# A two-layer hybrid decoder step: queries and keys stored by heads in DRAM, and the mixer's norm, bonus and gate made a stream of their own

## The chip, the core and the metric

The kernel runs as one program on one core of a Trainium2 chip. Five engines work beside each other and are tied by semaphores: TensorE (PE, with its weight loads as PEld), VectorE (DVE), ScalarE (ACT), GpSimd (POOL) and SyncE (SP), which here only issues DMAs. The metric is the device time of one execution in microseconds, lower is better. The granted clock is the share of TensorE's full clock that the chip gave (1.0 is 2.4 GHz, 0.5 is 1.2 GHz).

## The reference, cut to what matters

A prompt of 1024 positions and eight decode rows pass through two layers. In each layer one projection gives eight attention heads and eight RWKV-7 heads, whose outputs are joined, projected, normed and sent through a feed-forward block.

```python
def hybrid_layer(x, pos, x_prev, wkv0, kv_buf, v_first, lp):
    p = x @ lp['w_in']                       # q|k|v of 8 heads x 64, then r|k|v and LoRA columns
    q, k, v = ...                            # (B, T, 8, 64) each
    q, k = rope(q, pos), rope(k, pos)        # rotates the two 32-halves of each head
    att = dilated_attention_prompt(q, k, v)  # windows/dilations (128,1),(512,4),(2048,16), merged
    att = att * rsqrt(mean(att**2, -1) + RMS_EPS) * lp['att_gain']
    z = token_shift(p[..., ATT_COLS:], ...)
    rw, v_first, S_T = rwkv7_time_mix(z, v_first, wkv0, lp)
    mix = concatenate([att, rw], -1) @ lp['w_out']
    x1 = layer_norm(ALPHA * x + mix, ...)
    h = square(relu(x1 @ lp['w_ff_up'])) @ lp['w_ff_down']
    return layer_norm(ALPHA * x1 + h, ...), ...

def rwkv7_time_mix(z, v_first, wkv0, lp):
    ...
    g = sigmoid(g_lo) @ lp['gate_up']                       # gate
    def step(S, inp):                                       # per position, state S 64 x 64 per head
        sa = einsum('bhvk,bhk->bhv', S, a_t)
        S = S * w_t + sa * b_t + v_t * k_t                  # outer products
        return S, einsum('bhvk,bhk->bhv', S, r_t)
    S_T, y = lax.scan(step, wkv0, xs)
    y = (y - mean(y)) * rsqrt(var(y) + GN_EPS) * gn_g + gn_b   # per head: the norm
    y = (y + sum(r * k * bonus_rk, -1) * v) * g                # bonus, gate
    return y, v_first, S_T
```

## The kernel before, in words

**Halves and pairs.** Positions are cut into two halves of 512 (h = 0, 1; the decode rows ride with h = 1), and heads into four pairs p of 128 partitions (two heads of 64). The work of a layer l and half h is: the projection (`in_proj`), attention for four pairs, the RWKV mixer for four pairs in units of 256 positions (two units u per pair, 32 units in all, numbered s), then `half`: output projection, layer norm, feed-forward, layer norm.

**Dense work.** Every dense product is done in three passes (tiles xh/xl or hh/hl times wh/wl, lines 370 to 372, PSUM tile `dps`), in three PSUM banks tagged "d". ACT makes wh from each raw weight tile (line 343) and DVE makes wl (line 344); ACT also issues the weight loads.

**The order of PE's work** is written out when the program is built. Streams (Python generators) hand in pieces with a planned cost, a planned hold on a PSUM bank and a planned latency. `Streams.step` multiplies holds and latencies by a stream's slack: 1.2 in its first half-layer, 2.2 later (`SLK`, read through `R.phase`, which a stream sets by `R.enter`; a stream that never does so keeps 1.2). `Streams.run` always takes the first stream in the list that is ready at the planned time; dense work stands last and fills the rest. PE executes this list in order. The other engines' orders are chosen by the tile scheduler, and they too run in order: an instruction that waits holds up all behind it on its engine, and on SP a DMA that waits holds up all DMAs behind it.

**PSUM banks.** "r": one bank, for the mixer's second stage; "o": two, for that stage's outputs; "d": three, dense; "a": two, attention, the mixer's first stage and the rest.

**The mixer.** `stage1` makes a unit's operands: gates, norms, the decay products (AR, Wd), the triangular matrices (LB), and their inverse, for which POOL solves 16 x 16 blocks (lines 1209, 1211) between two trips through DRAM (`d_el`). It also makes the bonus term bv. `stage2` finishes the inverse (T1, pX: bank r), forms the products pO in the two o banks, and runs the chain over four blocks of 64 positions (St, pz, Z: bank r). Its last part is the norm, bonus and gate of y: `pgm` (the mean over each head, and the gate's product from `gs` and `gup`), `pgv` (the variance), three DVE operations and the store to `d_rw`, with both PE pieces in bank r. `stage1` of unit s starts after that last part of unit s-2 (note "u2").

**Attention's operands.** `in_proj` brings queries and keys (tile `qe`) out of PSUM in an order of partitions that suits the rotation: first halves of both heads, then second halves. It stores them as they are in `d_qkv` (line 638, one DMA of 128 x 512). `att_load` fetches them for the next pair, 64 partitions at a time, and puts a head's two halves together through the access pattern of the load:

```python
def heads(src):
    return src.rearrange("(f d r) t -> d f r t", f=2, d=2)
def stage(src, hd, n):
    t = ap_.tile([128, HB], F32, tag="stg", bufs=2, name="stg")[:, :n]
    for x in range(2):
        S.dma_start(t[64 * x:64 * x + 64], heads(src)[hd])
    return t
```

Here d is the head, f the half of the head, r the row in it; `stg` has two buffers. Each `stg` is then copied by ACT (qS line 1522, kS line 1526) and subtracted from by POOL (qL line 1523, kS line 1527). In the second half `qf` and `kf` (lines 1514, 1515) are loaded in the same way.

Of the kernel before, what the change touches and what calls it, by code (L numbers as in the profile page):

```python
# [10 lines left out]
F32 = mybir.dt.float32  # L11
# [10 lines left out]
NB = 8  # L22
DEPTH = 2
# [224 lines left out]
def body(ctx, tc, I, O):  # L248
# [303 lines left out]
    def in_proj(l, h, hook=None, tail=None, then=None):  # L552
# [61 lines left out]
        for kind, p in proj_order()[1:]:  # L614
            if kind == "a" and p == 3 and then is not None:
                yield from then()
            for j in range(3):
                w = W.take()
                if kind == "z":
                    ev = z_ev(p, j)  # L620
                    for c0, n in ck:
                        yield from dense([(w, 128, c0, n)], K8, xhc, xlc, ev)
                    continue
                seq = (2 * l + h) * 4 + p
                if j == 1 and seq > 0:
                    yield after("post", seq - 1)
                t = ap_.tile([128, HN[1]], F32, tag="qe", bufs=2, name="qe")

                def eva(it, pt):
                    _, _, c0, n = it  # L630
                    (V.tensor_copy if c0 else A.copy)(t[:, c0:c0 + n], pt[:, :n])
                for c0, n in CK[h]:
                    yield from dense([(w, 128, c0, n)], K8, xhc, xlc, eva)
                if j == 0 and h == 1:
                    t8 = ap_.tile([128, 5, 8], F32, tag="t8", name="t8")
                if j < 2:
                    rope(t, HN[h], tabs)
                    S.dma_start(d_qkv[l][h][p, j], t[:, 0:HB])
                    if j == 1:
                        S.dma_start(O["k_p"][l, p, :, h * HB:h * HB + HB], t[:, 0:HB])  # L640
                if h == 1 and j == 0:
                    if p == 0:
                        sq[l] = (rq.tile([128, 4, 32], F32, tag="q2", name="q2"), rq.tile([128, 4, 8], F32, tag="kn", name="kn"))
                        G.memset(sq[l][0], 0.0)
                    G.memset(t8[:, 1:4, :], 0.0)
                    for hd in range(2):
                        G.tensor_scalar(sq[l][0][:, p, hd:16:2], t[:, HB:HN[1]], C("hm")[:, hd:hd + 1], None, op0=ALU.mult)
                elif h == 1:
                    G.tensor_scalar(t8[:, (0, 4)[j - 1], :], t[:, HB:HN[1]], 1.0, None, op0=ALU.mult)
                    if j == 1:  # L650
                        G.tensor_scalar(sq[l][1][:, p, :], t[:, HB:HN[1]], 1.0, None, op0=ALU.mult)
            if kind == "a":
                qe[seq] = (l, h, p, t, t8 if h == 1 else None)
                note("qe", seq)
            note(kind, l, h, p)
# [427 lines left out]
    def stage1(l, h, p, u, s, lw, out):  # L1083
# [46 lines left out]
        if last:  # L1130
            yield (430, ("a", 1100), 0, "a")
            decode_terms(l, p, th, dup)
            yield (400, ("a", 700), 2000, "a")
        else:
            yield (860, ("a", 1100), 2000, "a")
        pb = bank("a", "pn")
        PE.matmul(pb[:, :n], C("blk"), sq, start=True, stop=True)
        if last:
# [102 lines left out]
            PE.transpose(pb[:, cc * 128:cc * 128 + 128], AR[:, tb, o:o + 128], ident)  # L1241
        A.copy(TV[:, :, :, 0, :], pb.rearrange("p (c h x) -> p c h x", c=4, h=2))
        yield (440, ("a", 900), 0, "a")
        pb = bank("a", "pbn")
        PE.matmul(pb[:, :n], C("blk"), bp, start=True, stop=True)
        bv = tmp("bv", bufs=2)
# [33 lines left out]
                    PE.matmul(pb[r, o + i * 64:o + i * 64 + 64], lt, rh, start=True, stop=True)  # L1280
        return pb[:, o:o + 256].rearrange("p (i t) -> p i t", t=64)

    def stage2(l, h, p, u, s, st, Z, Zp, gup, gs):

        AR, Wd, LB, TV, X, XT, bv, _ = st

# [84 lines left out]
        if h == 1 and u == NU - 1:  # L1371
            yield (200, ("r", 650), 900, "r")
            pz = bank("r", "pzf")
            for hd in range(2):
                hs = slice(64 * hd, 64 * hd + 64)
                PE.matmul(pz[hs, 0:64], Z[hs, :], istk[hs, :], start=True, stop=True)
            PE.matmul(pz[:, 64:72], gup, gs[:, UN:UN + NB], start=True, stop=True)
            Zo = rp.tile([128, 64], F32, tag="Zo", name="Zo")
            V.tensor_copy(Zo, pz[:, 0:64])
            S.dma_start(O["wkv_p"][l, 0, 2 * p:2 * p + 2].rearrange("h v k -> (h v) k"), Zo)  # L1380
            V.tensor_copy(dd["gsd"][:, p, :], pz[:, 64:72])
        yield (300, ("r", 700), 1500, "r")
        pb = bank("r", "pgm")
        PE.matmul(pb[:, 0:256], C("blk"), y, start=True, stop=True)
        PE.matmul(pb[:, 256:512], gup, gs[:, 0:256], start=True, stop=True)
        V.scalar_tensor_tensor(y, pb[:, 0:256], -1.0 / 64, y, op0=ALU.mult, op1=ALU.add)
        gg = rq.tile([128, 4, 64], F32, tag="T1", name="gg").rearrange("p a b -> p (a b)")
        A.copy(gg, pb[:, 256:512])
        sq = rq.tile([128, 4, 128], F32, tag="FG", name="gq").rearrange("p a b -> p (a b)")[:, 0:256]
        A.activation(sq, y, AF.Square)  # L1390
        yield (860, ("r", 1000), 1800, "r")
        pb = bank("r", "pgv")
        PE.matmul(pb[:, 0:256], C("blk"), sq, start=True, stop=True)
        A.activation(sq, pb[:, 0:256], AF.Ln, bias=epsc[:, 1:2], scale=1.0 / 64)
        A.activation(sq, sq, AF.Exp, scale=-0.5)
# [1 line left out]
        V.scalar_tensor_tensor(y, y, pv(l, "gnb", p), bv[:, 0:256], op0=ALU.add, op1=ALU.add)  # L1397
        V.tensor_tensor(y, y, gg, op=ALU.mult)
        S.dma_start(d_rw[l][h][p, :, u * UN:u * UN + UN], y)
        yield (430, ("r", 2000), 0, None)  # L1400

    def unit(l, h, p, u):
        return ((l * 2 + h) * 4 + p) * NU + u

    units = {}

    def stage1_stream():
        for l in range(DEPTH):
            for h in range(2):
                R.enter("s1", 2 * l + h)  # L1410
                yield after("lo", l, h, lat=3500)
                yield after("init")
                if h == 1:
                    for nm, k in (("dvt", 5), ("bvd", 4)):
                        dd[nm] = rq.tile([128, k, 8], F32, tag=nm, name=nm)
                for p in range(4):
                    yield after("z", l, h, p, lat=3500)
                    pc = slice(128 * p, 128 * p + 128)
                    dup = rp.tile([65, 128], F32, tag="dup", name="dup")
                    S.dma_start(dup[0:64, :], I["decay_up"][l, :, pc])  # L1420
                    S.dma_start(dup[64:65, :], I["decay_base"][l:l + 1, pc])
                    iup = rp.tile([128, 128], F32, tag="iup", name="iup")
                    S.dma_start(iup[64:128, :], I["iclr_up"][l, :, pc])
                    if l > 0:
                        S.dma_start(iup[0:32, :], I["vres_up"][l - 1, :, pc])
                    for u in range(NU):
                        s = unit(l, h, p, u)
                        if s >= 2:
                            yield after("u2", s - 2)
                        out = []  # L1430
                        yield from stage1(l, h, p, u, s, (dup, iup), out)
                        units[s] = out[0]
                        R.times["s1", s] = max(out[0][-1], R.now + 2000)
                if h == 1:
                    yield from decode(l)
                    note("dec", l)

    def stage2_stream():
        Zp = rp.tile([128, 4, 64], F32, tag="Zp", name="Zp")
        for l in range(DEPTH):  # L1440
            for h in range(2):
# [1 line left out]
                if h == 1:  # L1443
                    dd["gsd"] = rq.tile([128, 4, 8], F32, tag="gsd", name="gsd")
                for p in range(4):
                    gup = rp.tile([128, 128], F32, tag="gup", name="gup")
                    for u in range(NU):
                        s = unit(l, h, p, u)
                        yield after("s1", s)
                        if u == 0:  # L1450
                            S.dma_start(gup, I["gate_up"][l, :, 128 * p:128 * p + 128])
                        n = HN[h] - u * UN if u == NU - 1 else UN
                        gs = rp.tile([128, 264], F32, tag="gs", name="gs")
                        S.dma_start(gs[:, :n], d_lo[l][h][2, :, u * UN:u * UN + n])
                        yield (0, None, 0, "r")
                        yield from stage2(l, h, p, u, s, units.pop(s), None if h == 0 and u == 0 else Zp[:, p, :], Zp, gup, gs)
                        note("u2", s)
                    note("s2", l, h, p)

    def att_stream():  # L1460
# [27 lines left out]
    def att_load(l, h, p):  # L1488
# [2 lines left out]

        qS, qL, kS = [], [], []

        def heads(src):
            return src.rearrange("(f d r) t -> d f r t", f=2, d=2)

        def stage(src, hd, n):
            t = ap_.tile([128, HB], F32, tag="stg", bufs=2, name="stg")[:, :n]
            for x in range(2):
                S.dma_start(t[64 * x:64 * x + 64], heads(src)[hd])  # L1500
            return t

        def byres(t):
# [5 lines left out]
        qf = kf = None  # L1509
        if h == 1:  # L1510
            qf, kf = (ap_.tile([128, HB], F32, tag=x, name=x) for x in ("qf", "kf"))
            for hd in range(2):
                hs = slice(64 * hd, 64 * hd + 64)
                S.dma_start(qf[hs], heads(d_qkv[l][1][p, 0])[hd])
                S.dma_start(kf[hs], heads(d_qkv[l][0][p, 1])[hd])
        for hd in range(2):
            hs, ls = slice(64 * hd, 64 * hd + 64), slice(64 - 64 * hd, 128 - 64 * hd)
            q = ap_.tile([128, HB], F32R, tag=f"q{hd}", name="qS")
# [271 lines left out]

    R.work = WORK
    R.add("s2", stage2_stream(), SLK)
    R.add("s1", stage1_stream(), SLK)
    R.add("att", att_stream(), SLK)
    R.add("post", post_stream(), SLK)
# [64 lines left out]
```

## Time and profile before

| | |
|---|---|
| median of 3 runs | 3555.35 us (3549.26 to 3558.99) |
| profiled execution | 3560.94 us, its span 3559.1 us |
| mean granted TensorE clock | 0.949 |
| PE busy | 3202.7 us (90%) |
| DVE, ACT, POOL busy | 2055.5 us (58%), 1448.3 us (41%), 979.3 us (28%) |
| DMA queue q1 (SP's) | 245064 packets, 175.92 MB |

A row of a view of groups has the line of the kernel, engine, operation, tiles written and read, shapes, count, and times; a bracket at the end of a row of the timeline is the idle time of that engine just before the instruction and what ended it. "SPq" and "ACTq" are the engines' queues that issue DMAs.

### The profile page before, as it was taken

To read this page: it belongs to the slowest core of one execution; us is meant where nothing else is said; L and a number is where in the kernel's file an instruction comes from. 1 tells how busy PE (TensorE), PEld (TensorE's weight loads), DVE (VectorE), ACT (ScalarE), POOL (GpSimd) and SP (SyncE) were. 2 spreads that over 40 slices of the span, in tenths; PEclk is the share of its full clock that TensorE was granted. 3 is DMA by queue.
4 is the path that set the end of the run, shared out by engine and by line. 5 is a ranking of instruction groups with operands and counts; after the bars stand their busy time and mean duration, and the time that the engine had idled before them with its cause. 6 is when DMAs were issued, how large, how long until landed. Compare 5 with 4: busy or idle time off the path is not lost. (4 is left out here: it accounts for less than half of the span.)

```text
span 3559.1 us, 65853 instructions
## 1 busy us (share of the span) xinstructions
PE 3202.7 (90%) x24732; PEld 2697.6 (76%) x24732; DVE 2055.5 (58%) x4703; ACT 1448.3 (41%) x3266; POOL 979.3 (28%) x1841
## 2 busy tenths in 40 slices
PE   8788897977999998888999999797797999889998
PEld 6567776765777687677899998685675677789998
DVE  4455554764554664567565457465764564685556
ACT  4345333443343344344443336343443333453334
POOL 2324233531111421435211113334412121340012
PEclk9899998988999999998999999898898999999999
DMA  7334343433443335442333235344243343333332
GB/s 219 107 113 124 115 115 103 129 95 99 117 112 85 106 97 163 139 150 68 86 98 92 80 98 154 117 126 133 71 118 100 111 113 91 117 101 91 94 90 84
DMA packets 366533, 393.55 MB, mean 111 GB/s; under 512 B 141848, under 2 KB 219112, under 8 KB 366216
## 3 DMA queue, kind: packets, MB, share of 16 engines
q10 hardware_dynamic: 121152, 213.44, 20.9%
q1 hardware_dynamic: 245064, 175.92, 16.9%
q8 instruction: 195, 3.19, 0.4%
q14 instruction: 122, 1.00, 0.1%
HBM read 325.30 MB, written 63.97 MB: 109 GB/s over the span
## 5 line engine op out<-in xcount | busy, mean ns | idle before, releaser
L370 PE MATMUL dps<-xh,wh 128*128 128x256 f32 (+3 forms) x2984 | 1006.9, 337 | 31.0 <-ACT xh L758 15.0
L371 PE MATMUL dps<-xl,wh 128*128 128x256 f32 (+3 forms) x2984 | 956.8, 321 | 10.4 <-DVE xl L759 8.6
L372 PE MATMUL dps<-xh,wl 128*128 128x256 f32 (+3 forms) x2984 | 953.3, 319 | 1.2 <-DVE wl L344 1.0
L344 DVE TENSOR_TENSOR wl<-wr,wh 128x512 fp32r<-128x512 f32 (+1 forms) x772 | 581.8, 755 | 501.3 <-ACT wh L343 485.6
L343 ACT CAST wh<-wr 128x512 fp32r<-128x512 f32 (+1 forms) x772 | 475.1, 616 | 844.4 <-PE dps L371 777.8
L370 PEld LDWEIGHTS dps<-xh,wh 128*128 128x128 f32 x2984 | 576.6, 193 | 106.4 <-issue 31.0
L371 PEld LDWEIGHTS dps<-xl,wh 128*128 128x128 f32 x2984 | 576.8, 193 | 46.3 <-DVE xl L759 12.5
L372 PEld LDWEIGHTS dps<-xh,wl 128*128 128x128 f32 x2984 | 575.6, 193 | 41.0 <-DVE wl L344 2.6
L370 PE MATMUL dps<-hh,wh 128*128 128x512 f32 (+2 forms) x1600 | 536.1, 335 | 5.4 <-DVE hh L941 3.6
L371 PE MATMUL dps<-hl,wh 128*128 128x512 f32 (+2 forms) x1600 | 513.1, 321 | 4.5 <-DVE hl L830 3.3
L372 PE MATMUL dps<-hh,wl 128*128 128x512 f32 (+2 forms) x1600 | 512.0, 320 | 0.0
L370 PEld LDWEIGHTS dps<-hh,wh 128*128 128x128 f32 x1600 | 303.5, 190 | 45.2 <-issue 17.7
L371 PEld LDWEIGHTS dps<-hl,wh 128*128 128x128 f32 x1600 | 304.1, 190 | 22.6 <-DVE hl L830 4.1
L372 PEld LDWEIGHTS dps<-hh,wl 128*128 128x128 f32 x1600 | 303.9, 190 | 22.6
L1209 POOL TENSOR_TENSOR tm<-BL,XB 32x15 f32<-32x15 f32 (+7 forms) x480 | 153.0, 319 | 496.5 <-DMA BL<-d_el 375.9
L973 DVE TENSOR_TENSOR t<-dps,t 128x256 f32<-128x256 f32 (+1 forms) x240 | 123.6, 515 | 161.1 <-PE dps L372 160.7
L1211 POOL TENSOR_TENSOR XB<-XB,tm 32x15 f32<-32x15 f32 (+7 forms) x480 | 154.6, 322 | 34.4
L726 POOL TENSOR_TENSOR ln<-ln,lsq 128x256 f32<-128x256 f32 (+1 forms) x112 | 91.2, 814 | 232.5 <-ACT lsq L724 229.9
L941 DVE CAST hh<-rl 128x256 fp32r<-128x256 f32 (+2 forms) x200 | 74.4, 372 | 108.6 <-ACT rl L940 105.4
L939 ACT ACTIVATE rl<-dps 128x256 f32<-128x256 f32 (+2 forms) x200 | 88.4, 442 | 102.2 <-PE dps L372 89.9
L715 POOL TENSOR_TENSOR t<-t,ln 128x256 f32<-128x256 f32 (+1 forms) x32 | 28.1, 913 | 352.1 <-ACT ln L709 352.1
L370 PE MATMUL dps<-hh,xh 128*128 128x256 f32 (+1 forms) x368 | 112.6, 306 | 13.3 <-DVE t L1006 7.2
(345 smaller groups left out, 5098.0 us busy)
## 6 DMA issues: line engine op xcount, KB each, us to landing
wr<-in_w_ff_up ACTq DMA_DIRECT2D x272, 256.0 KB
wr<-in_w_ff_down ACTq DMA_DIRECT2D x256, 256.0 KB
wr<-in_w_in ACTq DMA_DIRECT2D x220, 256.0 KB
stg<-d_qkv SPq DMA_DIRECT2D x128, 128.0 KB
wr<-in_w_out ACTq DMA_DIRECT2D x64, 256.0 KB
z<-d_z SPq DMA_DIRECT2D x24, 384.0 KB
d_qkv<-qe SPq DMA_DIRECT2D x32, 256.0 KB
kvc<-in_cache_k SPq DMA_DIRECT2D x32, 256.0 KB
```

The lines of the kernel that those rows point to most:

```text
L343: self.copies.append(A.copy(h[:, :, :m], w[:, :, :m]))
L344: V.tensor_tensor(lo[:, :, :m], w[:, :, :m], h.bitcast(F32)[:, :, :m], op=ALU.subtract)
L370: PE.matmul(p[:m, :n], wh[:, wk % 4, :m], hi, start=(i == 0), stop=False)
L371: PE.matmul(p[:m, :n], wh[:, wk % 4, :m], lo, start=False, stop=False)
L372: PE.matmul(p[:m, :n], wl[:, wk % 4, :m], hi, start=False, stop=(i == last))
L715: G.tensor_tensor(t, t, self.cm[:, c0:c0 + n], op=ALU.subtract)
L726: G.tensor_tensor(s2, s2, sq, op=ALU.add)
L939: A.activation(r, p[:, :n], AF.Relu)
L941: V.tensor_copy(hh[:, c0:c0 + n], r)
L973: V.tensor_tensor(to, p[:, :n], to, op=ALU.add)
L1209: G.tensor_tensor(tv, bc(BL[:, 17 * j + 1:17 * j + 2], [(1, m), (0, j + 1)]), bc(XB[:, 16 * j:16 * j + 1], [(0, m), (1, j + 1)]), op=ALU.mult)
L1211: G.tensor_tensor(xv, xv, tv, op=ALU.add)
```

## The change

Two things are changed. First, the store of rotated queries and keys is cut into four DMAs of 32 partitions each, which put the two halves of a head beside each other in DRAM; the loads of `stg` then read 64 rows that lie together, and `qf` and `kf` are one load of 128 rows each. Second, the norm, bonus and gate leave `stage2` and become a generator `normed`, driven by a new stream "norm" that stands behind "s2" in the list and takes banks tagged "o" instead of "r". The end of the chain of unit s is noted as "ch". `stage1` no longer waits for "u2" of unit s-2 at its start; it waits for "ch" of s-2 before it writes AR and Wd and for "u2" of s-2 before it writes bv. The gate is copied into `gs` in place of a buffer of its own. The norm stream never calls `R.enter`.

```diff
                 if j < 2:
                     rope(t, HN[h], tabs)
-                    S.dma_start(d_qkv[l][h][p, j], t[:, 0:HB])
+                    for f in range(2):
+                        for d in range(2):
+                            a, b = 64 * f + 32 * d, 64 * d + 32 * f
+                            S.dma_start(d_qkv[l][h][p, j, b:b + 32], t[a:a + 32, 0:HB])
@@ stage1
+        if s >= 2:
+            yield after("ch", s - 2)
+            yield (0, None, 0, "a")
         pb = bank("a", "pn")
...
+        if s >= 2:
+            yield after("u2", s - 2)
+            yield (0, None, 0, "a")
         pb = bank("a", "pbn")
@@ stage2
-            PE.matmul(pz[:, 64:72], gup, gs[:, UN:UN + NB], start=True, stop=True)
...
-        yield (300, ("r", 700), 1500, "r")
-        pb = bank("r", "pgm")
+        ys[s] = (y, bv)
+        note("ch", s)
+        yield (300, ("r", 700), 500, None)
+
+    def normed(l, h, p, u, s, gup, gs):
+
+        y, bv = ys.pop(s)
+        yield (0, None, 900, "o")
+        pb = bank("o", "pgm")
         PE.matmul(pb[:, 0:256], C("blk"), y, start=True, stop=True)
         PE.matmul(pb[:, 256:512], gup, gs[:, 0:256], start=True, stop=True)
         V.scalar_tensor_tensor(y, pb[:, 0:256], -1.0 / 64, y, op0=ALU.mult, op1=ALU.add)
-        gg = rq.tile([128, 4, 64], F32, tag="T1", name="gg").rearrange("p a b -> p (a b)")
+        if h == 1 and u == NU - 1:
+            yield (860, ("o", 1000), 0, "o")
+            pz = bank("o", "pgd")
+            PE.matmul(pz[:, 0:8], gup, gs[:, UN:UN + NB], start=True, stop=True)
+            V.tensor_copy(dd["gsd"][:, p, :], pz[:, 0:8])
+        gg = gs[:, 0:256]
         A.copy(gg, pb[:, 256:512])
...
-        yield (860, ("r", 1000), 1800, "r")
-        pb = bank("r", "pgv")
+        yield (860, ("o", 1000), 1800, "o")
+        pb = bank("o", "pgv")
...
-        yield (430, ("r", 2000), 0, None)
+        yield (430, ("o", 2000), 0, None)
@@ stage1_stream
-                        if s >= 2:
-                            yield after("u2", s - 2)
@@
+    def norm_stream():
+        for l in range(DEPTH):
+            for h in range(2):
+                yield after("lo", l, h, lat=3500)
+                for p in range(4):
+                    for u in range(NU):
+                        s = unit(l, h, p, u)
                         if u == 0:
+                            gup = rp.tile([128, 128], F32, tag="gup", name="gup")
                             S.dma_start(gup, I["gate_up"][l, :, 128 * p:128 * p + 128])
                         n = HN[h] - u * UN if u == NU - 1 else UN
                         gs = rp.tile([128, 264], F32, tag="gs", name="gs")
                         S.dma_start(gs[:, :n], d_lo[l][h][2, :, u * UN:u * UN + n])
-                        yield (0, None, 0, "r")
-                        yield from stage2(l, h, p, u, s, units.pop(s), None if h == 0 and u == 0 else Zp[:, p, :], Zp, gup, gs)
+                        yield after("ch", s)
+                        yield from normed(l, h, p, u, s, gup, gs)
                         note("u2", s)
+                        yield (0, None, 3000, None)
                     note("s2", l, h, p)
@@ att_load
-        def heads(src):
-            return src.rearrange("(f d r) t -> d f r t", f=2, d=2)
...
-                S.dma_start(t[64 * x:64 * x + 64], heads(src)[hd])
+                S.dma_start(t[64 * x:64 * x + 64], src[64 * hd:64 * hd + 64])
...
-            for hd in range(2):
-                hs = slice(64 * hd, 64 * hd + 64)
-                S.dma_start(qf[hs], heads(d_qkv[l][1][p, 0])[hd])
-                S.dma_start(kf[hs], heads(d_qkv[l][0][p, 1])[hd])
+            S.dma_start(qf, d_qkv[l][1][p, 0])
+            S.dma_start(kf, d_qkv[l][0][p, 1])
@@
     R.add("s2", stage2_stream(), SLK)
+    R.add("norm", norm_stream(), SLK)
     R.add("s1", stage1_stream(), SLK)
```

How the instructions stand is shown at two places. The first is SP's queue where the second half's operands of the first pair are stored and loaded; a row gives the tiles and the size of the destination. Before:

```order
L638 DMA d_qkv_109<-qe 128x512
L1092 DMA lo_5113<-d_lo_104 128x2x256
L1514 DMA qf<-d_qkv_109 64x1x512 x2
L1500 DMA stg<-d_qkv_109 64x1x512 x2
L1500 DMA stg<-d_qkv_108 64x1x128 x2
L638 DMA d_qkv_109<-qe 128x512
L640 DMA out_k_p<-qe 128x512
L1500 DMA stg<-d_qkv_109 64x1x512 x4
```

The same place in SP's queue of the changed kernel:

```order
L641 DMA d_qkv_109<-qe 32x512 x4
L1525 DMA stg<-d_qkv_109 64x512
L1537 DMA qf<-d_qkv_109 128x512
L1525 DMA stg<-d_qkv_109 64x512
L1221 DMA d_el_118<-XB 32x16x16
L1222 DMA d_el_119<-tm 32x16x16
L1525 DMA stg<-d_qkv_108 64x128 x2
L1226 DMA X<-d_el_118 64x4x64
L1227 DMA XT<-d_el_119 64x4x64
```

One store of 128 rows became four of 32, two loads of `qf` became one, and the loads of `stg` lost a dimension of their pattern.

The second place is PE at the end of the chain of the ninth unit, the first of layer 0's second half (`pT` and `pBV` are the start of the next unit's second stage, `po`, `pS` and `pET` attention, `dps` dense work, `pn` the next but one unit's first stage). Before:

```order
L1384 MATMUL pgm<-y,cst 128x256
L1385 MATMUL pgm<-gs,gup 128x256
...
L1611 MATMUL po<-ET,vT 64x128 x6
L1554 MATMUL pS<-kf,qf 32x128 x4
...
L1393 MATMUL pgv<-gq,cst 128x256
...
L1280 MATMUL pT_7896<-X,LB 64x64 x8
L1280 MATMUL pBV<-TV,LB 64x64 x8
```

The same unit's end on PE in the changed kernel:

```order
L1398 MATMUL pgm<-y,cst 128x256
L1399 MATMUL pgm<-gs,gup 128x256
L1289 MATMUL pT_7004<-X,LB 64x64 x8
L1289 MATMUL pBV<-TV,LB 64x64 x8
L1143 MATMUL pn<-sq,cst 128x256
L1151 MATMUL pn<-cst,sg 128x128 x2
L370 MATMUL dps<-xh_89,wh 128x256
L371 MATMUL dps<-xl_91,wh 128x256
L372 MATMUL dps<-xh_89,wl 128x256
L1412 MATMUL pgv<-gq,cst 128x256
```

Before, 68 rows of PE lie between the second `pgm` row and `pT` of the next unit (`pgv` among them); now `pT` stands directly behind `pgm`, and `pgv` follows with six rows in between, the start of the next unit among them. In dense `dps` rows the mixer's work of a half-layer now ends earlier.

## Rows read from the trace of the kernel before

**Rows 1.** the page: busy time, share of the span and instructions of each engine.

```profile
PE 3202.7 (90%) x24732; PEld 2697.6 (76%) x24732; DVE 2055.5 (58%) x4703; ACT 1448.3 (41%) x3266; POOL 979.3 (28%) x1841
```

**Rows 2.** who PE waited for over the span: us in total, times, longest.

```profile
PE pz L1363 <- DVE St L1358: 26.4, 8, 13.1
...
PE pX L1280 <- ACT T L1302: 24.6, 5, 15.4
PE pds L1744 <- DMA kvc<-in_cache_k: 22.5, 1, 22.5
PE pbn L1245 <- ACT LB L1230: 22.3, 3, 8.9
...
PE pgv L1393 <- ACT gq L1390: 9.7, 4, 5.0
...
PE pT L1280 <- ACT gq L1394: 6.1, 1, 6.1
```

**Rows 3.** PE's timeline: start, us, line, tiles, and in brackets the idle time before.

```profile
269.41 1.12 PE L1588 MATMUL pET<-cst,E 128*128 128x128 f32 x4 [5.54 <-ACT LB L1230]
...
728.94 1.12 PE L1280 MATMUL pX<-XT,T 64*64 64x64 f32 x16 [15.38 <-ACT T L1302]
...
2414.10 1.12 PE L1342 MATMUL pO<-LB,TV 128*64 128x128 f32 x8 [14.16 <-ACT TV L1325]
...
2708.56 0.48 PE L1363 MATMUL pz<-cst,St 64*64 64x64 f32 x4 [5.10 <-DVE St L1358]
```

**Rows 4.** ACT's timeline, just ahead of those waits.

```profile
268.19 0.62 ACT L1526 CAST kS<-stg 128x512 fp32r<-128x512 f32 x1 [4.21 <-DMA stg<-d_qkv]
...
721.17 0.62 ACT L1526 CAST kS<-stg 128x512 fp32r<-128x512 f32 x1 [11.23 <-DMA stg<-d_qkv]
...
727.53 1.09 ACT L1522 CAST qS<-stg 128x512 fp32r<-128x512 f32 x1 [5.42 <-DMA stg<-d_qkv]
...
2411.87 1.09 ACT L1522 CAST qS<-stg 128x512 fp32r<-128x512 f32 x1 [15.25 <-DMA stg<-d_qkv]
```

**Rows 5.** the instructions of tile stg, and who waited for them (us, times).

```profile
L1500 SPq DMA_DIRECT2D stg<-d_qkv x160: 482/509/3642, 75.5 to 2698.1; - x160
...
  ACT kS L1526: 191.7, 33
...
  ACT qS L1522: 120.7, 19
```

**Rows 6.** windows: busy us (count) of each engine, then clock, DMA share, GB/s.

```profile
711.00:716.00 5.00, 2.56 (x17) 1.91 (x16) 1.12 (x4) 0.00 (x0) 0.00 (x0) 1.00 0.13 49
716.10:733.20 17.10, 4.26 (x43) 4.14 (x44) 3.76 (x5) 6.02 (x15) 5.71 (x6) 0.50 0.28 89
2402.30:2419.40 17.10, 5.30 (x34) 4.31 (x35) 3.43 (x8) 2.92 (x6) 3.71 (x3) 0.50 0.27 85
```

**Rows 7.** pieces of the chain that ended last: start, us, what.

```profile
2236.54 3.04 DMA d_qkv<-qe
2241.29 12.67 DMA stg<-d_qkv
...
2698.09 7.96 DMA stg<-d_qkv
...
2855.60 2.18 DMA d_el<-LB
...
2893.37 3.29 DMA ST<-in_state_wkv
```

**Rows 8.** PE's timeline at its longest wait.

```profile
888.65 1.73 PE L1744 MATMUL pds<-kvc,q 128*32 128x256 f32 x8 [22.53 <-DMA kvc<-in_cache_k]
```

**Rows 9.** SP's timeline ahead of it.

```profile
869.11 6.83 SPq L1500 DMA_DIRECT2D stg<-d_qkv  x4
876.04 3.68 SPq L1722 DMA_DIRECT2D kvc<-in_cache_k  x2
```

**Rows 10.** tile d_qkv: issue of the store on SP, ns min/median/max.

```profile
L638 SPq DMA_DIRECT2D d_qkv<-qe x32: 319/332/2788, 73.4 to 2430.7; - x32
```

More of the change, by code (lines that the diff above doesn't have):

```diff
@@ L1281, in small, with stage2 @@
         return pb[:, o:o + 256].rearrange("p (i t) -> p i t", t=64)
-    def stage2(l, h, p, u, s, st, Z, Zp, gup, gs):
+    def stage2(l, h, p, u, s, st, Z, Zp):
         AR, Wd, LB, TV, X, XT, bv, _ = st
@@ L1380, in stage2 @@
             S.dma_start(O["wkv_p"][l, 0, 2 * p:2 * p + 2].rearrange("h v k -> (h v) k"), Zo)
-            V.tensor_copy(dd["gsd"][:, p, :], pz[:, 64:72])
-        yield (300, ("r", 700), 1500, "r")
-        pb = bank("r", "pgm")
+        ys[s] = (y, bv)
[5 more added lines that the diff above has]
+        pb = bank("o", "pgm")
         PE.matmul(pb[:, 0:256], C("blk"), y, start=True, stop=True)
@@ L1399, in stage2 @@
         S.dma_start(d_rw[l][h][p, :, u * UN:u * UN + UN], y)
-        yield (430, ("r", 2000), 0, None)
+        yield (430, ("o", 2000), 0, None)
     def unit(l, h, p, u):
         return ((l * 2 + h) * 4 + p) * NU + u
-    units = {}
+    units, ys = {}, {}
     def stage1_stream():
@@ L1445, in stage2_stream @@
                 for p in range(4):
-                    gup = rp.tile([128, 128], F32, tag="gup", name="gup")
                     for u in range(NU):
@@ L1449, in stage2_stream @@
                         yield after("s1", s)
+                        yield (0, None, 0, "r")
+                        yield from stage2(l, h, p, u, s, units.pop(s), None if h == 0 and u == 0 else Zp[:, p, :], Zp)
+    def norm_stream():
[5 more added lines that the diff above has]
+                        s = unit(l, h, p, u)
                         if u == 0:
+                            gup = rp.tile([128, 128], F32, tag="gup", name="gup")
                             S.dma_start(gup, I["gate_up"][l, :, 128 * p:128 * p + 128])
```

## The prediction

> **What bounds the kernel now.** I read the page's busy times first: PE is busy for 3202.7 us of the span of 3559.1 us [rows 1], so 356 us of it is idle, and no other engine is over 58%. The order of PE is fixed, so the question is which arrivals PE stands still for. The list of PE's waits shows them spread over a dozen causes of 5 to 26 us each, nearly all of them small copies on ACT or DVE of under a microsecond that release a step of the mixer [rows 2]. A copy that short doesn't explain a wait of 15 us, so I went to the timeline of PE at each long wait, and to that of ACT just ahead of it. There the cause is one and the same. PE waits 15.38 us at 728.94, 14.16 us at 2414.10, 5.54 us at 269.41 [rows 3]; just before, ACT stood still for 11.23 and 5.42 us, for 15.25 us and for 4.21 us, and each time for a load of `stg`, attention's queries and keys [rows 4]. ACT runs in order: the mixer's copy that PE needs stands behind attention's copy, which waits for its load. I found fourteen such pairs in PE's timeline, from 269.41 to 2708.56 (the least is 4.75 us); their PE waits add up to 125.5 us. Over the span ACT waits 191.7 + 120.7 us for `stg` in 52 places [rows 5]; the rest falls where PE had other work. The longest wait of all, 22.53 us at 888.65, is for a decode load [rows 8]; on SP it was issued at 876.04, behind four loads of `stg` whose issue alone took 6.83 us [rows 9]. I count it with the others: 148 us of the 356.
>
> Why is a load of 128 KB so slow? In a stretch in which SP's queue moved little else, the DMA engines were busy for 0.13 of their time, which is two of sixteen, and moved 49 GB/s [rows 6]. At that rate a load of 128 KB takes 2.7 us, and a pair's eight (first half) or sixteen (second half, four of them smaller) queue up on the same two engines. In the chain that ended last such a load takes from 7 to 15 us; the chain has ten pieces of `stg`, between 2241.29 and 2698.09, with 102 us together, 10.2 us each [rows 7].
>
> **The change part by part.**
>
> *Loads by heads.* The pattern of the load loses its outer dimension of two and becomes 64 rows that lie together. The trace has no load of `stg` in that form. The nearest row is `ST`, of the same size, with 64 partitions of 2 KB: 3.29 us from issue to landing; a smaller one with 64 partitions took 2.18 us [rows 7]. So I take 3.3 us in place of 10.2, and the bounds are 10.2 (no better) and 2.2. Of a wait that is made of such loads 1 - 3.3/10.2 = 68% then falls away: 0.68 x 148 = 100 us. Bounds: 0, and 0.78 x 148 = 116 us, or all 148 if what stays is hidden.
>
> The DMA page of the Trainium skill (DMA: Bandwidth & Descriptors, "Why a DMA increments its semaphore by 16 and not by 1") says how many engines a DMA gets: the largest number up to 16 that divides the slowest dimension of both sides. By that rule the old pattern, whose source begins with a dimension of two, has two engines, and the new one sixteen. The share of 0.13 agrees for the old one; no row here shows `stg` in the new one, and by the rule alone the 2.7 us of moving would be 0.3 us and the gain at the upper bound.
>
> *The clock.* Where PE stands still the granted clock falls to 0.50: around two of the waits a stretch of 17.1 us runs at 1.2 GHz, with 4.26 and 5.30 us of PE work in it [rows 6]. At the other level that work takes half, so 2.1 to 2.7 us go with a long wait. Fifteen waits at 2.4 us give 36 us at most; most are shorter, with shorter stretches, and a third of the waiting stays, so I take 15 us, with bounds 0 and 36.
>
> *Stores in four pieces.* 32 stores become 128. An issue takes 0.33 us on SP [rows 10], so 96 more take 32 us of a queue that blocks on other things far longer, while 16 loads of `qf` and `kf` go and the issue of `stg` (0.51 us [rows 5]) may shorten. A load that waits for the store waits for the last of four: three more issues, 1 us, against 3.04 us for the old store in one piece [rows 7]. I cost it at nothing; uncovered, it is 1 us in each of 32 stores, 32 us.
>
> The same page ("Bandwidth") speaks against this part: it wants large DMAs, says that transfers under 64 KB are made of descriptors' cost, and gives each a fixed cost of about 2 us. If the four paid that one after the other, a store would take 8 us and not 3, 5 us in 32 places. The rows allow for less, since a landed piece of 2.18 us and issues of 0.33 us overlap; no run here shows the four together.
>
> *The norm stream.* PE's work stays the same; its order changes. The two pieces `pgm` and `pgv` leave the one r bank, so the next unit's `pT` stands directly behind `pgm`. What can go is the wait of `pT` for the last norm (6.1 us) and those at `pgv` (9.7 us) [rows 2], and of these some are already among the fourteen: at best 10 us. What can come: `pgv` has 7 rows of PE's order between it and `pgm` instead of 26, the start of the next unit among them, and a planned latency at slack 1.2 in all half-layers (2.2 before in three of four). The longest wait at `pgv` so far is 5.0 us [rows 2]; every one of 32 units at that price is 160 us. And the planner packs the mixer closer: counted in dense products, the second half of layer 0 has its eight units within 1581 instead of 1863, 15% less. Idle time that isn't `stg`'s is 356 - 148 = 208 us, mostly the mixer's; 15% of it is 31 us. I take +31 us for the stream as a whole, between -10 and +160, near the low end because waits at `pgv` cost 9.7 us in all so far, 0.3 us per unit. What is late next on PE is the chain itself: `pz` behind St, 26.4 us in eight places, 13.1 us of it in one of the fourteen [rows 2].
>
> *Sum.* 3560.9 (the profiled execution) - 100 - 15 + 31 = 3477. The median of the runs is 5.6 us under that execution, so 3471 us, 2.4% less.
>
> **The rivals.**
>
> *The load is fast, but ACT waits for something else.* Two buffers of `stg` serve a chain of load, copy, subtraction on POOL; the next load can't start before POOL is done, and ACT's order still has attention's copies ahead of the mixer's. If half the gain goes this way: -50 - 7 + 31 = -26, about 3529 us. For it: ACT's waits were planned against some latency, and POOL is slow. Against: the waits themselves name the DMA, not POOL [rows 4, 5].
>
> *All of it goes.* What stays of the waits is hidden and the stream costs nothing: -148 - 36 = -184, 3371 us; the middle of this case, half way from my forecast, is about 3420 us. For it: without stalls of ACT the clock stays up and nothing queues. Against: PE's order is fixed, and behind each wait something is next.
>
> *The loads stay slow.* Then only the stream counts: 3555 - 10 to 3555 + 31, around 3570 us. For it only that no load of this tile in the new form has been seen; against it `ST` [rows 7].
>
> *Slower.* The norm's steps on PE, planned too tight, wait in every unit, at `pgv` and at the o banks that `pO` of the next unit then finds occupied. Against the gain of 115 us it decides from 3.6 us per unit (115/32); at 5.0 us per unit, the longest so far, it is +160 - 115 = +45, 3600 us. For it: the lower slack in three half-layers, and in-order queues on ACT and DVE that now carry two units at once. Against: in the first half-layer the slack was 1.2 before as well, and the waits at `pgv` have come to 9.7 us in all.
>
> **How the numbers follow.** The forecast (3435 to 3515 us) has a chance of 0.50, the case in which all goes 0.16, the halved gain 0.20, loads that stay slow 0.05, slower 0.09. A difference under 0.3%, 11 us, can't be told from none. The halved gain is faster in nine of ten; slow loads are within 0.3% in half the cases, slower in the rest. Faster: 0.50 + 0.16 + 0.18 = 0.84; same: 0.02 + 0.03 = 0.05; slower: 0.09 + 0.02 = 0.11. The range reaches to 3400 us, which takes in the nearer part of the case in which all goes, and to 3540 us, which takes in the halved gain.
>
> **What would show it.** Right: ACT's waits for `stg` fall from 312 us to under 100, the windows with loads of `stg` show more than 0.13 of the DMA engines for a shorter time, PE's waits over 10 us are gone, PE's idle time is near 290 us and the mean granted clock above 0.949. The norm shows in PE's waits at `pgv`, `pgm` and `pO`: under 40 us together the stream is cheap, over 115 us it has eaten the gain. My forecast is wrong if ACT still waits 10 us for `stg`, or if PE's idle time stays at 356 us with other names in it.

## The result, and the profile after

The changed kernel takes 3303.61 us (3300.99 to 3313.16), the kernel before 3555.17 us: a ratio of 0.9299 (95% interval 0.9276 to 0.9321), 252 us less. I had forecast 84 us less and a range down to 3400 us, so the direction was right and the size wrong by a factor of three; even the case in which all of the counted waits go, 3371 us, was too slow.

From the page of the changed kernel, first the row that answers to [rows 1], then the granted clock in 40 slices, in tenths:

```profile
PE 3148.5 (95%) x24732; PEld 2658.2 (81%) x24732; DVE 2052.6 (62%) x4703; ACT 1446.9 (44%) x3266; POOL 981.6 (30%) x1841
...
PEclk9999999999999999999999999999999999999999
```

PE is idle for 3298.9 - 3148.5 = 150 us of the span, against 356 [rows 1]: 206 us less. PE's busy time is 54 us shorter for the same 24732 matmuls, and the mean granted clock is 0.982 against 0.949. These two, 206 and 54 us, make up the 260 us by which the span of the profiled execution is shorter.

PE's list of waits (us in total, times, longest), for [rows 2]:

```profile
PE pz L1372 <- DVE St L1367: 9.4, 6, 2.3
PE pgv L1412 <- ACT gq L1409: 9.1, 6, 4.4
...
PE pS L1577 <- DVE dms L1801: 5.3, 1, 5.3
...
PE pdo L1799 <- DMA kvc<-in_cache_v: 3.7, 3, 1.7
...
PE pT L1289 <- DVE mx L1596: 0.4, 1, 0.4
...
PE pbn L1254 <- ACT LB L1236: 0.3, 1, 0.3
```

The wait of `pX` for the copy T (24.6 us before) and that of `pds` are not in the list any more, that of `pbn` is down from 22.3 to 0.3 us, and `pz` behind St from 26.4 to 9.4 us with 2.3 as the longest. No wait is over 5.3 us, where the longest before were 15.4 and 22.5 us. At `pgv` there are 9.1 us against 9.7.

The tile `stg`: first the load's issue, then who waited for it, for [rows 5]:

```profile
L1525 SPq DMA_DIRECT2D stg<-d_qkv x160: 444/540/2155, 75.8 to 2479.9; - x160
...
  ACT kS L1549: 43.9, 20
...
  ACT qS L1545: 14.7, 9
```

ACT's waits for the loads fell from 312.4 to 58.6 us. What a load does now is seen in a window in which SP's queue alone moved anything (columns as in [rows 6]), and in pieces of the chain that ended last, for [rows 7]:

```profile
2183.00:2185.00 2.00, 2.00 (x33) 1.53 (x27) 0.78 (x4) 0.00 (x0) 0.00 (x0) 1.00 0.88 261
```

```profile
2052.29 3.25 DMA d_qkv<-qe
2056.73 4.20 DMA stg<-d_qkv
...
2182.18 3.87 DMA stg<-d_qkv
...
2325.12 3.76 DMA stg<-d_qkv
...
2336.03 2.63 DMA stg<-d_qkv
```

The DMA engines are busy for 0.88 of the stretch and move 261 GB/s, where they were at 0.13 and 49 GB/s. A piece of `stg` in the chain takes 2.6 to 4.2 us; the four have a mean of 3.6. The 3.25 us of the store are those of one of its four pieces. SP's timeline has the issues ahead of it:

```profile
2051.29 1.90 SPq L641 DMA_DIRECT2D d_qkv<-qe  x4
```

The first piece is issued at 2051.29, and the piece that the chain waits for, issued at 2052.29, lands at 2055.54. So from the first issue the store takes 4.25 us here, against 3.04 in one piece [rows 7].

### The profile page after: what moved, and what is told of

The parts are those of the page before. It is cut to its first block, busy times and chain, and to the rows that moved or that the text cites. A ratio compares the mean times of both kernels' runs of the same rounds, so it can differ in the third digit from the quotient of the medians.

```text
span 3298.9 us, 65922 instructions
## 1 busy us (share of the span) xinstructions
PE 3148.5 (95%) x24732; PEld 2658.2 (81%) x24732; DVE 2052.6 (62%) x4703; ACT 1446.9 (44%) x3266; POOL 981.6 (30%) x1841
## 5 line engine op out<-in xcount | busy, mean ns | idle before, releaser
L370 PE MATMUL dps<-xh,wh 128*128 128x256 f32 (+3 forms) x2984 | 996.2, 334 | 21.2 <-ACT xh L761 7.4
L344 DVE TENSOR_TENSOR wl<-wr,wh 128x512 fp32r<-128x512 f32 (+1 forms) x772 | 572.0, 742 | 369.7 <-ACT wh L343 350.7
L370 PEld LDWEIGHTS dps<-xh,wh 128*128 128x128 f32 x2984 | 567.5, 190 | 97.4 <-issue 28.7
L371 PEld LDWEIGHTS dps<-xl,wh 128*128 128x128 f32 x2984 | 568.6, 191 | 43.7 <-DVE xl L762 10.3
L372 PEld LDWEIGHTS dps<-xh,wl 128*128 128x128 f32 x2984 | 568.2, 190 | 39.9 <-DVE wl L344 2.7
L370 PE MATMUL dps<-hh,wh 128*128 128x512 f32 (+2 forms) x1600 | 529.5, 331 | 4.7 <-DVE hh L944 3.6
L372 PEld LDWEIGHTS dps<-hh,wl 128*128 128x128 f32 x1600 | 301.7, 189 | 22.3
L718 POOL TENSOR_TENSOR t<-t,lnm 128x256 f32<-128x256 f32 (+1 forms) x80 | 72.5, 939 | 300.3 <-ACT lnm L712 294.3
```

The source lines that it names most:

```text
L344: V.tensor_tensor(lo[:, :, :m], w[:, :, :m], h.bitcast(F32)[:, :, :m], op=ALU.subtract)
L370: PE.matmul(p[:m, :n], wh[:, wk % 4, :m], hi, start=(i == 0), stop=False)
L371: PE.matmul(p[:m, :n], wh[:, wk % 4, :m], lo, start=False, stop=False)
L372: PE.matmul(p[:m, :n], wl[:, wk % 4, :m], hi, start=False, stop=(i == last))
L718: G.tensor_tensor(t, t, self.cm[:, c0:c0 + n], op=ALU.subtract)
```

## The experiments

Theory A: the loads with an outer dimension of two are the whole cause, by more ways than the fourteen waits that I counted. Rival B: they are worth my 115 us, and the norm stream brings the rest. All ratios are to the kernel before on the same chip.

**The layout alone.** The kernel before with the diff's lines on `d_qkv`, `stage`, `qf` and `kf`, and nothing else.

> The kernel before with only the new layout of queries and keys (four stores of 32 rows, loads of 64 rows that lie together); the norm stays in the second stage on bank r. Theory A (the loads on two DMA engines cost nearly all of the 252 us, directly and through all else that stood behind them): about 3330 us, PE idle near 170 us. Rival B (the loads are worth the 115 us that I forecast, the norm stream the rest): about 3440 us.

Measured: 3300.51 us, ratio 0.9255 (0.9241 to 0.9268). The page's row of busy times and ACT's waits for `stg` in this kernel:

```profile
PE 3148.5 (96%) x24732; PEld 2658.7 (81%) x24732; DVE 2064.1 (63%) x4703; ACT 1449.8 (44%) x3266; POOL 979.5 (30%) x1841
```

```profile
  ACT kS L1524: 36.2, 21
  ACT qS L1520: 17.4, 11
```

PE is idle for 3296.0 - 3148.5 = 147.5 us and ACT waits 53.6 us. All of the gain is here, and it goes beyond what A had said (3330 us, 170 us of idle time); B falls.

**The norm stream alone.**

```diff
-                    for f in range(2):
-                        for d in range(2):
-                            a, b = 64 * f + 32 * d, 64 * d + 32 * f
-                            S.dma_start(d_qkv[l][h][p, j, b:b + 32], t[a:a + 32, 0:HB])
+                    S.dma_start(d_qkv[l][h][p, j], t[:, 0:HB])
...
-                S.dma_start(t[64 * x:64 * x + 64], src[64 * hd:64 * hd + 64])
+                S.dma_start(t[64 * x:64 * x + 64], heads(src)[hd])
```

> The changed kernel with the old store and the old loads, so only the norm stream is new. Theory A: 3530 to 3590 us, ACT still waits about 300 us for the loads. Rival B: about 3420 us, since the stream would bring some 130 us by itself. A third theory, C (the two parts only work together): both this and the layout alone give less than half of the 252 us.

Measured: 3578.56 us, ratio 1.0039 (1.0026 to 1.0052): slower by 0.4%. The wait at `pgv` in this kernel:

```profile
PE pgv L1409 <- ACT gq L1406: 34.8, 11, 14.1
```

It went from 9.7 to 34.8 us. With fast loads the same stream has 9.1 us there, so most of it belongs to ACT's stalls. Theory C, by which the two parts only work together, falls with this run and the one before.

**The old layout with loads cut in two.**

```diff
-                S.dma_start(t[64 * x:64 * x + 64], heads(src)[hd])
+                for f in range(2):
+                    o = 64 * x + 32 * f
+                    S.dma_start(t[o:o + 32], src[64 * f + 32 * hd:64 * f + 32 * hd + 32])
```

> The kernel before with its old store and layout; each load of 64 rows is cut into two of 32 rows that lie together, so there are twice as many loads (320 of stg, 64 of qf and kf), none with an outer dimension of two. If the pattern of the load is the cause, as A says, it comes within 40 us of the kernel with the new layout alone; if the number of issues on SP or the layout in DRAM matters, it stays over 3450 us.

Measured: 3297.44 us, ratio 0.9246 (0.9232 to 0.9260), the same as the new layout within the intervals, although 160 loads became 320. So neither the place of the halves in DRAM nor the number of issues makes the difference; what the two kernels share is that no load has an outer dimension of two. Both this kernel and the layout alone are ahead of the changed kernel.

**The changed kernel with loads on two engines again.**

```diff
+    d_qk = both(lambda l, h: dr.tile([4, 2, 4, 33, HB], F32, name=f"d_qk{l}{h}"))
...
-                S.dma_start(t[64 * x:64 * x + 64], src[64 * hd:64 * hd + 64])
+                S.dma_start(t[64 * x:64 * x + 64], src[2 * hd:2 * hd + 2, 0:32])
```

> The changed kernel with a gap of one row behind each 32 rows of queries and keys in DRAM, so that the loads have an outer dimension of two again; stores stay in four pieces and the norm stream stays. Theory A: the loads move at about 49 GB/s again, ACT waits about 300 us for them, and the time is that of the norm stream alone, 3530 to 3590 us. Rival B: about 3420 us.

Measured: 3578.83 us, ratio 1.0031 (1.0020 to 1.0043). The gap of one row behind each 32, which gives the loads an outer dimension of two again, takes the whole gain back. A window with loads alone, and ACT's waits:

```profile
2578.00:2581.00 3.00, 0.00 (x0) 0.00 (x0) 0.00 (x0) 0.00 (x0) 0.00 (x0) 0.50 0.13 49
```

```profile
  ACT kS L1552: 195.4, 34
...
  ACT qS L1548: 112.5, 20
```

**The layout alone, with loads on four engines.** DRAM in groups of 16 rows with a gap behind each, on the kernel with the new layout alone, so that the loads have an outer dimension of four. Each store is cut into eight pieces of 16 rows, which the lines below do not show.

```diff
+    d_qk = both(lambda l, h: dr.tile([4, 2, 8, 17, HB], F32, name=f"d_qk{l}{h}"))
...
-                S.dma_start(t[64 * x:64 * x + 64], src[64 * hd:64 * hd + 64])
+                S.dma_start(t[64 * x:64 * x + 64], src[4 * hd:4 * hd + 4, 0:16])
```

> The kernel before with queries and keys in DRAM in groups of 16 rows with a gap of a row behind each (eight stores of 16 rows each), so the loads have an outer dimension of four. If a load takes the engines its outer dimension allows, it moves at about 98 GB/s and the waits shrink by more than half, since queues drain faster than they fill: 3340 to 3420 us, ACT waits 100 to 150 us for stg. If only a pattern without any gap is fast, it stays at 3560 us; if two was a special case, it is at 3300 us.

Measured: 3399.06 us, ratio 0.9523 (0.9508 to 0.9538). A window of loads, and ACT's waits:

```profile
2534.00:2537.00 3.00, 3.00 (x28) 2.21 (x26) 0.00 (x0) 1.16 (x2) 0.46 (x1) 1.00 0.27 100
```

```profile
  ACT kS L1528: 84.4, 27
  ACT qS L1524: 69.1, 21
```

Twice the share of the engines (0.27), twice the rate (100 GB/s), half the wait (153.5 us, a little over the 150 expected). Times sixteen engines, the shares for outer dimensions of 2, 4 and 64 are 2.1, 4.3 and 14.1 engines. What the four additional pieces of each store cost in this run was not separated.

**Attention's copies on POOL.** The kernel before, with its slow loads.

```diff
-            A.copy(inrow(q), byres(t))
+            G.tensor_scalar(inrow(q), byres(t), 1.0, None, op0=ALU.mult)
...
-                A.copy(k[:, c:c + n], t)
+                G.tensor_scalar(k[:, c:c + n], t, 1.0, None, op0=ALU.mult)
```

> The kernel before with its loads on two engines; the copies qS and kS of attention's operands are made by POOL instead of ACT, so ACT never waits for stg. Theory A1 (the loads cost time because ACT runs in order and holds the mixer's copies behind attention's): PE's waits behind ACT go, about 3420 us, though POOL has 80 us more to do and its solve of the 16 x 16 blocks now stands behind the loads. Rival A2 (the loads hold up the other DMAs of SP's queue, and those hold PE): over 3520 us.

Measured: 3576.45 us, ratio 1.0015 (1.0005 to 1.0025). POOL's waits for `stg`, and three of PE's waits:

```profile
  POOL kS L1526: 177.6, 27
  POOL qS L1522: 88.4, 16
```

```profile
PE pT L1280 <- DMA X<-d_el: 37.2, 10, 15.0
PE pS L1565 <- POOL kS L1527: 33.0, 4, 19.7
...
PE lnq L740 <- POOL ln L726: 14.8, 4, 10.9
```

ACT never waits for `stg` now, but POOL waits 266 us, and what stands behind it on POOL (the solve that `pT` needs through X, the rest of `kS`, the layer norm's sums) holds PE too. POOL also has 115 us more to do (1094.6 against 979.3 us). My expectation of 3420 us was wrong; by the mark that I had set, over 3520 us, the run came out as A2 had it. But PE's order is that of the kernel before, so the same instructions can be looked up, here those of two waits of [rows 3]:

```profile
710.13 0.68 PE L1280 MATMUL pX<-XT,T 64*64 64x64 f32 x16
...
2406.47 0.66 PE L1342 MATMUL pO<-LB,TV 128*64 128x128 f32 x8
```

The waits of 15.38 and 14.16 us are gone, although the loads are as slow and on the same queue as before. Over the twenty long waits that the next section compares, the idle time fell from 177.6 to 43.5 us; at all other instructions it rose from 168 to 317 us. So ACT's order did hold PE at those places, as A1 says, and the same total (1.0015) comes of new waits elsewhere. How much the other DMAs of SP's queue held PE, this run doesn't separate.

**The slow loads from POOL's queue.** `G.dma_start` in place of `S.dma_start` for `stg`, `qf` and `kf`.

> The kernel before with the loads of stg, qf and kf in their old form, issued by POOL's queue instead of SP's. If most of the time goes because other DMAs of SP's queue stand behind these loads (A2), this gains over 80 us although the loads themselves are as slow; if the engine that waits for the loads is what holds PE (whichever it is), the time stays over 3520 us. If loads from POOL's queue are spread over more DMA engines, the waits for stg fall and the time goes towards 3300 us.

Measured: 3973.39 us, ratio 1.1148 (1.1133 to 1.1164). From the tile's view (POOL's idle time before it, then ACT's waits):

```profile
  issue: 556.8, 125
...
  ACT kS L1526: 388.2, 38
  ACT qS L1522: 223.0, 20
```

POOL stood idle for 557 us at the issues, and ACT's waits doubled to 611 us. From POOL's queue the loads came one at a time; a piece of POOL's timeline and the tile's times from issue to landing:

```profile
96.19 0.66 POOL L1500 DMA_DIRECT2D stg<-d_qkv  x1 [5.25 <-issue]
...
102.13 0.67 POOL L1500 DMA_DIRECT2D stg<-d_qkv  x1 [4.95 <-issue]
108.16 0.66 POOL L1500 DMA_DIRECT2D stg<-d_qkv  x1 [5.36 <-issue]
```

```profile
DMA to landing us min/median/max: 2.6/5.6/8.1
```

None of the 192 loads was issued before the one ahead of it had landed. A2's gain didn't come, but POOL's own stalls and the later loads are added here, so the run leaves open what the other DMAs alone would have gained.

**What the norm stream costs, on one chip.** The changed kernel and the layout alone.

> The changed kernel as it is, on one chip with the kernel that has the new layout alone (the next run); so far the two stood beside the kernel before on different chips, at 0.9299 and 0.9255. If the norm stream costs something on top of the fast loads too, this is 10 to 18 us slower than the next run; if the difference was one of chips, the two agree within 5 us.

> The new layout alone, as in e1_heads_only, beside the changed kernel on the same chip: ratio 0.9255 again; 10 to 18 us under the run above if the norm stream costs, equal to it if not.

Measured: 3319.88 us, ratio 0.9319 (0.9304 to 0.9333), and 3303.46 us, ratio 0.9269 (0.9255 to 0.9282). The norm stream costs 16 us, 0.5%, with fast loads too. In the profiled executions of these two runs PE has 156.2 us of idle time against 149.2, and 3159.5 us of busy time against 3150.5.

**Why it costs, three attempts.** Three edits of the changed kernel: `R.enter("norm", 2 * l + h)` in the norm stream; `if s >= 2: yield after("u2", s - 2)` put back ahead of `stage1`; every "o" in `normed` replaced by "r".

> The changed kernel in which the norm stream calls R.enter and so gets slack 2.2 after the first half-layer. The norm stream alone made the kernel 0.4% slower. If its tight planned latency is why (waits at pgv), this comes 8 to 15 us under the changed kernel, at a ratio near 0.926, with waits at pgv under 4 us in all; if the reason is the crowding of the mixer, it stays at 0.930.

> The changed kernel in which the first stage waits at its start for the norm of unit s-2 again, as before the change; norm stream and banks stay. If the earlier start of the first stage (a closer packed mixer) is what costs the 0.4%, this goes to a ratio near 0.926; if it is the norm's own steps, it stays at 0.930 or a little over.

> The changed kernel with the norm stream on bank r, as the norm was before, instead of the o banks. The stream costs 0.5% on top of the fast loads, and neither its slack nor the first stage's gate explains it. If the o banks are the reason (the products pO of the next unit find them held), this comes to a ratio of 0.925 to 0.928; if it is the stream's place in the order whatever the bank, it stays at 0.930 to 0.933.

Measured: 3313.98 us, ratio 0.9289 (0.9269 to 0.9310); 3316.74 us, 0.9291 (0.9269 to 0.9313); 3316.01 us, 0.9287 (0.9266 to 0.9308). With the higher slack PE's waits at `pgv` all but go:

```profile
PE pgv L1412 <- DVE kk L1163: 1.4, 1, 1.4
PE pgv L1412 <- ACT gq L1409: 1.3, 2, 0.9
```

Yet PE's idle time in that execution is 156.5 us, no less than in the changed kernel (150.4 and 156.2). By the time nothing is decided: all three ratios lie between the layout alone (0.9255 and 0.9269) and the changed kernel (0.9299 and 0.9319), were taken on other chips than these, and have intervals that touch both. Why the stream costs 0.5% stays open.

## Why the prediction was right in direction and wrong in size

**The load itself: right.** I took 3.3 us from the row of `ST`; pieces of `stg` in the chain now have a mean of 3.6 us. The rule of the Trainium skill that I weighed (DMA: Bandwidth & Descriptors, "Why a DMA increments its semaphore by 16 and not by 1") is borne out by the runs: outer dimensions of two, four and 64 gave shares of 0.13, 0.27 and 0.88.

**The stores: right.** With stores in four pieces (layout alone, 0.9255) and in one piece (old layout, loads cut in two, 0.9246) the time is the same within the intervals, although the second has twice as many loads; costed at nothing was right. The store looked at took 1.2 us more than in one piece (4.25 against 3.04), near the 1 us that I had worked out from the issues. The rule of the Trainium skill that spoke against the stores ("Bandwidth" of the same page) didn't decide. The fixed cost of about 2 us that I named beside it stands in another section of that page of the Trainium skill, "Anatomy of one DMA — SWDGE (gpsimd) path", for DMAs issued by GpSimd; the estimate from it, 8 us for four in a row, is not what the store took.

**The waits that go: the step that failed.** The term "0.68 x 148 = 100 us" should have been 209 us (356.4 - 147.5, the layout alone). PE's order is the same in the kernel before and in the layout alone (but for a few neighbours), so the idle time just before each instruction can be compared one by one. My fourteen waits are among nineteen of 4.75 us and more between 269.41 and 2708.56; with the decode load's these are twenty, 177.6 us together, and all other instructions have 168 us before them (the 11 us of the span after PE's last instruction are in neither). In the layout alone the same twenty come to 9.7 us. Three of them there, for the 15.38, 22.53 and 14.16 us of [rows 3] and [rows 8]:

```profile
614.94 0.68 PE L1283 MATMUL pX<-XT,T 64*64 64x64 f32 x16
...
755.41 0.63 PE L1742 MATMUL pds<-kvc,q 128*32 128x256 f32 x4 [3.60 <-DMA kvc<-in_cache_k]
...
2197.15 0.66 PE L1345 MATMUL pO<-LB,TV 128*64 128x128 f32 x8
```

So two things in the term were wrong. I let a third of each wait stay, 48 us, because the load still takes 3.3 us; of the counted 148 us at most 9.7 stayed. These waits weren't scaled by the duration of the load: in the layout alone only 32 of attention's 80 copies wait for `stg` at all, 1.7 us on average, where 52 waited before, 6.0 us on average. And I counted too few: the five long waits that I left out went too (about 30 us before), and the idle time at all other instructions fell from 168 to 127 us, 41 us more. I had written that the rest of ACT's 312 us "falls where PE had other work"; a part of it did, but not all. (One reading in the working was loose as well: of the chain's ten pieces of `stg` one took 4.84 us, not 7 or more; their sum is right.)

Taken together, ACT's wait and the time move almost as one: from 312.4 to 153.5 us of wait (four engines) the time falls by 171 us on that run's chip, and from there to 53.6 us (layout alone) by the difference of the two ratios, 0.0268, about 96 us. But the time holds the clock's part too, and with the copies on POOL ACT's wait was nothing and the time stayed. It is a sum that comes out, not a price.

Loads that are not `stg` land sooner too. SP's own waits for the two steps of the solve through DRAM, in the kernel before and in the layout alone:

```profile
SPq L1201 <- DMA d_el<-LB: 83.7, 36, 6.9
...
SPq L1220 <- DMA d_el<-XB: 39.7, 25, 6.7
```

```profile
SPq L1204 <- DMA d_el<-LB: 60.5, 39, 4.5
...
SPq L1223 <- DMA d_el<-XB: 37.2, 29, 2.7
```

The longest fall from 6.9 to 4.5 and from 6.7 to 2.7 us. I read it as these transfers no longer standing behind those of `stg` on two engines; no run shows that by itself. I had not counted this at all, and how much of the gain it is was not separated.

**The clock: right mechanism, mis-sized.** I took 15 us, 36 at most, from two stretches at 1.2 GHz with about 5 us of PE's work in each. PE's busy time fell by 54 us with the same matmuls. All stretches with a granted clock of 0.50 summed, in the kernel before (47 of them) and in the layout alone (25):

```profile
sum 361.45, PE 207.36; mean PE 4.41
```

```profile
sum 119.36, PE 99.98; mean PE 4.00
```

107 us of PE's work left the lower level. At the higher it takes half of that, 54 us, and 54 us is what PE's busy time lost. I had priced only the stretches at the fifteen waits, at most 72 us of such work; the stretches at shorter waits went too.

**The norm stream: right sign.** I took +31 us between -10 and +160; it costs 16 us (0.5%) on the fast loads and 12 us (0.4%) alone. The rival in which it is slower overall stayed far off: waits at `pgv` are 9.1 us in all (with `pgm` and `pO` under 40 us, as I had marked for a cheap stream), 0.3 us per unit, against the 3.6 us from which it would have decided. Whether its wording, too tight a latency, is the cause of the 16 us isn't decided: with slack 2.2 the waits at `pgv` fall to 2.7 us, and the ratio, 0.9289, lies between the two kernels. Nor is it shown that the closer packing of the mixer, from which I took the +31 us, is what costs; that the sign came out may be luck.

**The other rivals.** "ACT waits for something else" fell: ACT's waits for `stg` went from 312.4 to 58.6 us, and the time came out far under its 3529 us. "The loads stay slow" is what the two-engine run makes, and it gives 1.0031. "All of it goes" was the nearest, at 3371 us; it failed by the same undercount of waits and of clock. By my own marks, ACT's wait came out under 100 us and the mean clock over 0.949 as said; PE's idle time came to 150 us instead of 290.

## What to carry to other kernels

Look at the outermost dimension of a load's pattern in DRAM before its bytes. In windows where the queue moved only such loads, the busy share of the DMA engines times sixteen came to 2.1 and 4.3 for dimensions of two and four and to 14.1 for 64; a share that low in a stretch of loads is the sign to look for. When PE's order doesn't change, compare its idle time instruction by instruction: that shows which waits a change took, and here they went almost whole, the short ones with the long. Don't price a slow load only by the long waits that can be seen behind it: here the twenty longest gave 168 of 209 us. And split a change that does two things: here one part was worth 7.4% and hid that the other costs 0.5%.

## What the runs showed that I had not expected

Cutting each load in two (320 instead of 160 issues on SP) costs nothing that shows: 0.9246 against 0.9255. The same slow loads from POOL's queue went out one at a time, each after the one ahead had landed, and the kernel took 11% longer. And moving a blocking copy from ACT to POOL took away most of PE's long waits and brought as many others, at the same total time (1.0015).
